# A two-layer decoder trunk: attention pieces counted by matmuls, and stick-breaking sums in fewer, wider matmuls

## The chip, the cores and the metric

The kernel runs on one core of a Trainium2 chip. The metric is the device time of one execution in microseconds (us). The engines that matter are TensorE (PE in the rows; its weight loads are PEld), VectorE (DVE) and ScalarE (ACT). GpSimd (POOL) does very little, and SyncE (SP) only issues the loads of the weights.

## What is computed

`DEPTH` = 2 layers over 256 tokens of width 1024, in float32. A layer has one input projection for three attention branches with 8 heads each, and a squared-ReLU MLP:

```python
proj = hdn @ w_in[l]          # hdn: RMSNorm of x, scaled and shifted by the conditioning
q_lat, c_kv, k_pe, sb_qkv, mb_qkv, gates = split(proj)
q  = rmsnorm(q_lat) @ w_uq[l]      # 768 -> heads of 64 + 32 (rotary)
kv = rmsnorm(c_kv) @ w_ukv[l]      # 256 -> keys (64 a head) and values (64 a head)
o_mla = causal_softmax_attention(q, kv)       # branch A
o_sb  = stick_breaking_attention(sb_qkv)      # branch B
o_mb  = causal_softmax_attention(mb_qkv)      # branch C (at 256 tokens its one block is the own block)
x = x + gate1 * (sum of sigmoid(gates) * (o @ w_o)) @ w_out
x = x + gate2 * squared_relu(hdn2 @ w_ff1) @ w_ff2
```

Stick-breaking attention is `A[t,s] = exp(log_beta[t,s] + sum over s < j < t of log_keep[t,j])`: a sum over the later keys, for each query.

## The kernel before

Activations are held transposed, 128 features on the partitions and 256 tokens along the row. Every product is made of three matmuls on float32 split in a high and a low half (`mm3`, lines 325 to 327: high x high, high x low, low x high). A **job** is one tile of weights of 128 x 2048 at most: SyncE loads it into `ws`, ScalarE rounds it into `wh` (line 168), VectorE subtracts that for `wl` (line 170, 596 of 608 times), in four pieces. Its matmuls are divided into **parts**, most with 24 matmuls of 256 columns. The jobs of a layer, in order: `sb` and `mb` (queries, keys, values of branches B and C), `lat`, `kpe`, the gates of B, **`wukv`**, three jobs **`uq`**, the output projection `osb`, the gates of C, `omb`, the gates of A, `omla`, `wout`, and the MLP. Each third job or so a raw job is put between, in which VectorE makes a conditioning vector of the next section (line 225).

`wukv` has six parts: four make the keys (`ukv`, into the PSUM tile `kn`, copied to `km` by ScalarE at line 700) and two the values (`mla_v`, into `mvps`, copied at line 722). Each of these parts has only 6 matmuls, of 256 columns in `ukv` and of 512 in `mla_v`. A part of a `uq` job has 18, of an output projection 12.

Attention lies between the jobs. Each pair of heads is a Python generator, `sb_attn` or `sm_attn`, that issues a piece of work and then yields how many hand-overs to skip. `run` (line 202) goes through a job's parts; after each it calls `pump`, which lets the two oldest generators make their next piece or count down. For softmax (`sm_attn`) the pieces are: scores `s` with the mask (lines 495 to 501), row maxima and exponentials `e`; two hand-overs later the sums' reciprocals and the scaling of `e` on VectorE (line 518); three later six transposes into `pt` (lines 522 to 524) and the copy `pT`; two later the product with the values into `po` (`av`). For stick-breaking the scores `z` come first, then the log terms `l`, split in `lh` and `ll`; three hand-overs later the sums are added into `z` by matmuls with the triangle `upper` and with `neg_ones` (lines 482 to 486). `drain` in the first `omla` job finishes whatever is left. PSUM tiles of the jobs, `po`, `kn` and `mvps` share three buffers.

The program's order on each engine is made when it is built, and each engine then goes through its instructions in that order.

Of the kernel before, what the change touches and what calls it, by code (L numbers as in the profile page):

```python
# [32 lines left out]
SEAM_N = -3  # L33
WARM = 8, 4, 24
PHASE = 48


@with_exitstack
def trunk(ctx, tc, xT, heads, pos, signs, masks, vecs, gfin, wada, win, wkpe, wuq, wukv, wo, wout, wff1, wff2, out):
# [7 lines left out]
    def mmps(name):  # L47
        return psum.tile([128, 2, 256], F32, name=name, tag="mm", bufs=3)

    def atps(name):  # L50
        return psum.tile([128, 2, 512], F32, name=name, tag="at", bufs=2)
# [4 lines left out]
    def slot(name, dt=F32, shape=(128, 8, 256)):  # L56
        a, b = shape[1:]
        t = big.tile([128, PHASE + 8 * (S + 2)], dt, name=name, tag="slot", bufs=8)
        return t[:, PHASE:PHASE + a * b].rearrange("p (a b) -> p a b", b=b)

# [3 lines left out]
    def t768(name, dt=F32):  # L64
        return work.tile([128, 2, 384], dt, name=name, tag="t768", bufs=4)
# [3 lines left out]

    act = cpool.tile([128, PHASE + 2 * KT * S], F32R, name="act")  # L70
    hh, hl = (act[:, PHASE + i * KT * S:PHASE + (i + 1) * KT * S].rearrange("p (a b) -> p a b", b=S) for i in range(2))
    x = cpool.tile([128, KT, S], F32, name="x")
# [7 lines left out]
    upper, rot_m, rot_b = (csr[:, i, :] for i in range(3))  # L80
    neg_ones = cpool.tile([128, 128], F32R, name="negs")
# [48 lines left out]
    tc.no_sync_barrier()  # L130

    class Job:
        def __init__(self, src, f, parts, raw=False):
            self.src, self.f, self.parts, self.raw = src, f, parts, raw

    jobs = []
    side = []
    state = {"dma": 0, "split": 0, "auto": False}
    PIECES = 4

    def fetch(i):
# [33 lines left out]
    def split_to(i, pc):  # L175
        while state["split"] < min(PIECES * i + pc, PIECES * len(jobs)):
            split_piece()

    def later(i, n):
        while n and i + 1 < len(jobs):  # L180
            i += 1
            n -= not jobs[i].raw
        return i

    def pump():
        for g in list(side[:2]):
            if g[1] > 0:
                g[1] -= 1
                continue
            try:  # L190
                g[1] = next(g[0])
            except StopIteration:
                side.remove(g)
# [8 lines left out]
    def run(i):  # L202
        job = jobs[i]
        if job.raw:
            return
        split_to(i, PIECES)
        n = len(job.parts)
        a = state["split"]
        m = PIECES * (later(i, AHEAD) + 1) - a
        for j, part in enumerate(job.parts):  # L210
            split_to(0, a + m * j // n + (j == 0))
            part(job.wh, job.wl)
            split_to(0, a + m * (j + 1) // n)
            pump()

    def split(dh, dl, src):
        nc.scalar.activation(dh, src, AF.Copy)
        nc.vector.tensor_sub(dl, src, dh.bitcast(F32))  # L218
# [21 lines left out]
    def add_job(job):  # L240
        jobs.append(job)
        every["n"] += 1
        if pending and every["n"] > 0 and every["n"] % every["k"] == 0:
            jobs.append(pending.pop(0)[2])
# [79 lines left out]
    def mm3(o, wh, wl, ah, al, first, last):  # L324
        nc.tensor.matmul(o, wh, ah, start=first, stop=False)  # L325
        nc.tensor.matmul(o, wh, al, start=False, stop=False)  # L326
        nc.tensor.matmul(o, wl, ah, start=False, stop=last)  # L327

    def half(ps, i, wh, wl, kts, ncol, c, ah, al):
        for k in range(kts):  # L330
            c0 = k * ncol + c
            mm3(ps[:, i, :], wh[:, c0:c0 + 128], wl[:, c0:c0 + 128], ah[:, k, :], al[:, k, :],
                k == 0, k == kts - 1)
# [108 lines left out]
    def av(pT, v, p, oh, ol):  # L442
        po = mmps("po")
        for h in range(2):
            d = slice(64 * h, 64 * h + 64)
            vc = slice(p * 128 + 64 * h, p * 128 + 64 * h + 64)
            nc.tensor.matmul(po[d, 0, :], v[:, 0, vc], pT[:, h, 0:256], start=True, stop=False,  # L447
                             tile_position=(0, 64 * h))
        for h in range(2):
            d = slice(64 * h, 64 * h + 64)  # L450
            vc = slice(p * 128 + 64 * h, p * 128 + 64 * h + 64)
            nc.tensor.matmul(po[d, 0, 128:256], v[:, 1, vc], pT[:, h, 256:384], start=False, stop=True,
                             tile_position=(0, 64 * h))
        split(oh[:, p, :], ol[:, p, :], po[:, 0, :])

    def masked(ps, cols, mask, stop):
        nc.tensor.matmul(ps[:, cols], ident_b, mask, start=False, stop=stop, skip_group_check=True)

    def sb_attn(qk, v, p, out):
        z = atps("z")  # L460
        for s in range(2):
            for h in range(2):
                d = slice(64 * h, 64 * h + 64)
                q, k = qk[d, 2 * p, :], qk[d, 2 * p + 1, :]
                if s == 0:
                    nc.tensor.matmul(z[:, h, 0:256], k[:, 0:128], q, start=True, stop=False, skip_group_check=True)
                else:
                    nc.tensor.matmul(z[:, h, 256:384], k[:, 128:256], q[:, 128:256], start=False, stop=False,
                                     skip_group_check=True)
        for h in range(2):  # L470
            for c in (0, 256):
                masked(z[:, h, :], slice(c, c + 128), mask_sb, True)
        l = t768("l")
        zv = z[:, :, 0:384]
        nc.scalar.activation(l, zv, AF.Abs)
        nc.scalar.activation(l, l, AF.Exp, scale=-1.0)
        nc.scalar.activation(l, l, AF.Ln, bias=1.0)
        nc.vector.scalar_tensor_tensor(l, zv, 0.0, l, op0=OP.max, op1=OP.add)
        lh, ll = t768("lh", F32R), t768("ll", F32R)
        split(lh, ll, l)  # L480
        yield 2
        for h in range(2):
            for o, n, w, c in ((0, 256, upper, 0), (128, 128, neg_ones, 256), (256, 128, upper, 256)):
                for t in (lh, ll):
                    nc.tensor.matmul(z[:, h, o:o + n], w, t[:, h, c:c + n], start=False, stop=t is ll,
                                     skip_group_check=True)
        a = t768("a")
        nc.scalar.activation(a, zv, AF.Exp)
        yield 1
        av(a, v, p, *out)  # L490
# [60 lines left out]
    def layer(l):  # L551
# [23 lines left out]
        def start_sb():  # L575
            T["osb"] = otile("osb")
            for p in range(4):
                spawn(sb_attn(T["sbqk"], sbv["v"], p, T["osb"]))
# [125 lines left out]
        def ukv(j, i):  # L704
            def go(wh, wl):
                if i == 0:
                    cell["kn"] = mmps("kn")
                half(cell["kn"], i, wh, wl, 2, 1024, j * 256 + i * 128, T["lh"], T["ll"])
                if i == 1:
                    nope_done("km")(0)(cell["kn"], j)  # L710
            return go

        def mla_v(t):
            def go(wh, wl):
                if t == 0:
                    cell["mv"] = work.tile([128, 2, 512], F32, name="mv", tag="v", bufs=2)
                ps = mmps("mvps")
                for k in range(2):
                    s = slice(k * 1024 + 512, k * 1024 + 1024)
                    mm3(ps, T["lh"][:, k, t * 128:t * 128 + 128], T["ll"][:, k, t * 128:t * 128 + 128],  # L720
                        wh[:, s], wl[:, s], k == 0, k == 1)
                nc.scalar.activation(cell["mv"][:, t, :], ps.rearrange("p a b -> p (a b)"), AF.Copy)
            return go

        add_job(Job(wukv[l], 2048, [ukv(0, 0), ukv(0, 1), ukv(1, 0), ukv(1, 1), mla_v(0), mla_v(1)]))

        def qlat():
            return T["lh"][:, 2:8, :], T["ll"][:, 2:8, :]
# [225 lines left out]
    for l in range(L):  # L954
        layer(l)
# [84 lines left out]
    for i in range(6, len(jobs)):  # L1040
        for f in hooks.get(i, []):
            f()
        if i not in skip:
            run(i)
# [93 lines left out]
```

## Time and profile before

| | us |
|---|---|
| three timed runs | 952.01, 952.58, 953.62 (median 952.58) |
| the profiled execution | 952.03 |
| its span, first to last instruction | 950.2 |
| TensorE matmuls busy | 926.7 (98%), 7839 instructions |
| TensorE weight loads busy | 891.7 (94%) |
| VectorE busy | 742.6 (78%) |
| ScalarE busy | 608.0 (64%) |
| DMA queue q1, share of 16 engines | 60.8% |

The busy time of TensorE is made of matmuls that overlap: the shown duration of one is longer than its distance to the next. So what one costs is read from the starts of neighbours. The mean granted TensorE clock is 0.991 of full speed.

### The profile page before, as it was taken

What the parts mean: (1) busy time and instruction counts of PE and PEld (TensorE: products, weight loads), DVE (VectorE), ACT (ScalarE), POOL (GpSimd) and SP (SyncE); (2) the same over time, 40 slices, a digit from 0 to 9 for tenths busy, and PEclk for the clock granted to TensorE, in tenths of its full rate; (3) what the DMA queues carried; (4) which work ended last, traced back from release to release, by engine and by line L of the source; (5) the groups of instructions that cost most, each with busy time, mean ns of one, the idle gap of its engine ahead of it and who ended that gap; (6) DMA issues with size and microseconds to landing.
All of it is one profiled execution on the core that took longest, in us unless ns stands there. A gap on an engine that the chain in (4) does not pass through costs nothing.

```text
span 950.2 us, 19399 instructions
## 1 busy us (share of the span) xinstructions
PE 926.7 (98%) x7839; PEld 891.7 (94%) x7840; DVE 742.6 (78%) x1438; ACT 608.0 (64%) x1275; POOL 28.3 (3%) x27
## 2 busy tenths in 40 slices
PE   8889999999999999999999999999999999999996
PEld 4889999799999999999999999979999999999995
DVE  7969869797889887667797876979787998555554
ACT  5465678867676775646376657886867678464641
POOL 1510000000000000000000000000000000000002
PEclk9989999999999999999999999999999999999998
DMA  8957556565566488677866565556546647755531
GB/s 328 348 190 260 206 183 216 191 220 195 194 253 238 142 291 308 244 267 264 312 222 245 206 237 178 200 170 227 214 178 223 221 157 266 262 189 197 179 128 44
DMA packets 32920, 208.90 MB, mean 220 GB/s; under 512 B 3776, under 2 KB 4416, under 8 KB 9280
## 3 DMA queue, kind: packets, MB, share of 16 engines
q1 hardware_dynamic: 32688, 207.49, 60.8%
q8 instruction: 61, 1.00, 0.4%
q14 instruction: 27, 0.22, 0.1%
q0 software_dynamic: 144, 0.20, 0.1%
HBM read 206.62 MB, written 1.05 MB: 219 GB/s over the span
## 4 chain that ended last, share of the span: by engine, by line
PE 76%; DVE 15%; DMA 5%; ACT 2%; issue 1%; SPq 0%; DVEq 0%; ACTq 0%
PE ps L325 15%; PE ps L326 15%; PE ps L327 15%; DVE wl L170 5%; PE ff L907 4%; PE ff L910 4%; PE ff L908 4%; PE pre L347 4%; DVE adaw L225 2%; DVE ws L225 2%; DMA ws<-wada 2%; DMA ws<-wff 1%; PE po L447 1%; PE vps L325 1%; PE vps L327 1%
## 5 line engine op out<-in xcount | busy, mean ns | idle before, releaser
L170 DVE TENSOR_TENSOR wl<-ws,wh 128x512 fp32r<-128x512 f32 (+2 forms) x596 | 383.0, 676 | 135.5 <-ACT wh L168 134.8
L168 ACT ACTIVATE wh<-ws 128x512 fp32r<-128x512 f32 (+2 forms) x608 | 344.4, 610 | 194.1 <-PE ps L326 93.5
L325 PE MATMUL ps<-act,wh 128*128 128x256 f32 x1120 | 313.1, 280 | 0.0
L327 PE MATMUL ps<-act,wl 128*128 128x256 f32 x1120 | 310.5, 277 | 0.0
L326 PE MATMUL ps<-act,wh 128*128 128x256 f32 x1120 | 310.5, 277 | 0.0
L325 PEld LDWEIGHTS ps<-act,wh 128*128 128x128 f32 x1120 | 210.4, 188 | 1.3 <-issue 1.0
L326 PEld LDWEIGHTS ps<-act,wh 128*128 128x128 f32 x1120 | 211.2, 189 | 0.2
L327 PEld LDWEIGHTS ps<-act,wl 128*128 128x128 f32 x1120 | 210.2, 188 | 0.0
L907 PE MATMUL ff<-fh,wh 128*128 128x256 f32 x448 | 123.6, 276 | 0.0
L908 PE MATMUL ff<-fl,wh 128*128 128x256 f32 x448 | 123.6, 276 | 0.0
L910 PE MATMUL ff<-fh,wl 128*128 128x256 f32 x448 | 123.6, 276 | 0.0
L225 DVE SCALAR_TENSOR_TENSOR ws<-ws,cb 128x1024 f32<-128x1024 f32 x80 | 95.9, 1220 | 17.0 <-DMA ws<-wada 17.0
L908 PEld LDWEIGHTS ff<-fl,wh 128*128 128x128 f32 x448 | 84.1, 188 | 0.0
L907 PEld LDWEIGHTS ff<-fh,wh 128*128 128x128 f32 x448 | 84.1, 188 | 0.0
L910 PEld LDWEIGHTS ff<-fh,wl 128*128 128x128 f32 x448 | 84.1, 188 | 0.0
L318 ACT ACTIVATE act<-ht,mod 128x256 fp32r<-128x256 f32 x32 | 15.5, 506 | 30.4 <-DVE ht L317 30.4
L421 PE MATMUL first<-act,wh 128*128 128x256 f32 x128 | 27.6, 315 | 7.1 <-ACT act L318 4.6
L774 POOL TENSOR_SCALAR xg<-x,gf 128x256 f32<-128x256 f32 x8 | 8.2, 1033 | 882.4 <-ACT wh L168 873.4
L511 ACT ACTIVATE e<-s,st 128x128 f32<-128x128 f32 (+1 forms) x64 | 26.0, 421 | 11.1 <-DVE st L506 11.0
L421 PEld LDWEIGHTS first<-act,wh 128*128 128x128 f32 x128 | 23.2, 220 | 8.8 <-ACT act L318 5.5
L347 PE MATMUL pre<-xh,wh 128*128 128x258 f32 x96 | 28.3, 294 | 0.0
L326 PE MATMUL ps<-ml,wh 128*128 128x256 f32 x96 | 26.6, 280 | 0.8 <-DVE ml L218 0.8
(261 smaller groups left out, 1862.5 us busy)
## 6 DMA issues: line engine op xcount, KB each, us to landing
ws<-wff SPq DMA_DIRECT2D x64, 1024.0 KB, 4.9
ws<-win SPq DMA_DIRECT2D x50, 1024.0 KB, 4.9
ws<-wada SPq DMA_DIRECT2D x40, 1024.0 KB, 4.9
ws<-wo SPq DMA_DIRECT2D x12, 1024.0 KB, 4.8
adaw<-wada SPq DMA_DIRECT2D x8, 1024.0 KB, 9.1
ws<-wout SPq DMA_DIRECT2D x8, 1024.0 KB, 5.6
ws<-win SPq DMA_DIRECT2D x24, 256.0 KB, 7.9
ws<-wuq SPq DMA_DIRECT2D x6, 768.0 KB, 4.3
```

The source lines that it names most:

```text
L168: nc.scalar.activation(job.wh[:, a], job.ws[:, a], AF.Copy)
L170: eng.tensor_sub(job.wl[:, a], job.ws[:, a], job.wh[:, a].bitcast(F32))
L225: nc.vector.scalar_tensor_tensor(w, w, 1.0, cb, op0=OP.mult, op1=OP.mult, accum_out=mods[l][:, 2 * b + i:2 * b + i + 1])
L325: nc.tensor.matmul(o, wh, ah, start=first, stop=False)
L326: nc.tensor.matmul(o, wh, al, start=False, stop=False)
L327: nc.tensor.matmul(o, wl, ah, start=False, stop=last)
L347: nc.tensor.matmul(ps[:, i, 0:258], w[:, c:c + 128], a[:, k, :], start=k == 0 and n == 0, stop=k == KT - 1 and n == 2, skip_group_check=True)
L421: nc.tensor.matmul(ps[:, i, :], w[:, c:c + 128], a[:, k, :], start=i == 0 and k == 0 and n == 0, stop=k == KT - 1 and n == 2, skip_group_c ...
L511: nc.scalar.activation(e[:, h, a:b], s[:, h, a:b], AF.Exp, scale=scale, bias=st[:, 4 + c:5 + c], accum_out=st[:, 8 + c:9 + c])
L907: nc.tensor.matmul(o, wh[:, c0:c0 + 128], fh[:, k, :], start=st, stop=False, skip_group_check=True)
L908: nc.tensor.matmul(o, wh[:, c0:c0 + 128], fl[:, k, :], start=False, stop=False, skip_group_check=True)
L910: nc.tensor.matmul(o, wl[:, c0:c0 + 128], fh[:, k, :], start=False, stop=en, skip_group_check=True)
```

## The change

There are two edits. A job now knows how many matmuls a part of it has (24, and 6 for `wukv`); `run` adds them up after each part and hands over a piece when 12 have come together, and then starts again from zero. And in the stick-breaking sums the triangle is applied to columns 0 to 383 in one matmul, where it was applied to 0 to 255 and to 256 to 383 in two.

```diff
+PUMP = 12
@@ class Job
-        def __init__(self, src, f, parts, raw=False):
-            self.src, self.f, self.parts, self.raw = src, f, parts, raw
+        def __init__(self, src, f, parts, raw=False, mms=24):
+            self.src, self.f, self.parts, self.raw, self.mms = src, f, parts, raw, mms
@@ run
             part(job.wh, job.wl)
             split_to(0, a + m * (j + 1) // n)
-            pump()
+            state["mms"] += job.mms
+            if state["mms"] >= PUMP:
+                state["mms"] = 0
+                pump()
@@ sb_attn
-            for o, n, w, c in ((0, 256, upper, 0), (128, 128, neg_ones, 256), (256, 128, upper, 256)):
+            for o, n, w, c in ((0, 384, upper, 0), (128, 128, neg_ones, 256)):
                 for t in (lh, ll):
                     nc.tensor.matmul(z[:, h, o:o + n], w, t[:, h, c:c + n], start=False, stop=t is ll,
                                      skip_group_check=True)
@@ layer
-        add_job(Job(wukv[l], 2048, [ukv(0, 0), ukv(0, 1), ukv(1, 0), ukv(1, 1), mla_v(0), mla_v(1)]))
+        add_job(Job(wukv[l], 2048, [ukv(0, 0), ukv(0, 1), ukv(1, 0), ukv(1, 1), mla_v(0), mla_v(1)], mms=6))
```

Lines behind line 212 stand four lower after the change: line 700 of before is 704 of after.

On TensorE, the sums of one head in a stick-breaking pair, with the matmul ahead of them (`csr` holds the triangle, `negs` is `neg_ones`). Before:

```order
L327 MATMUL ps<-act,wl 128x256
L485 MATMUL z<-lh,csr 128x256
L485 MATMUL z<-ll,csr 128x256
L485 MATMUL z<-lh,negs 128x128
L485 MATMUL z<-ll,negs 128x128
L485 MATMUL z<-lh,csr 128x128
L485 MATMUL z<-ll,csr 128x128
```

and after the change:

```order
L331 MATMUL ps<-act,wl 128x256
L489 MATMUL z<-lh,csr 128x384
L489 MATMUL z<-ll,csr 128x384
L489 MATMUL z<-lh,negs 128x128
L489 MATMUL z<-ll,negs 128x128
```

The second head follows with the same rows, so a group of two heads has 12 matmuls before and 8 after; there are four groups in a layer.

On ScalarE, during `wukv` in layer 0 (the numbers tell the tiles of one name apart; `e_1989` and `e_2033` belong to the first and second pair of branch C). Before:

```order
L700 ACTIVATE km_1581<-kn_1998 64x256 x4
L128 ACTIVATE gate_1690<-gate_1690 128x512
L511 ACTIVATE e_1989,st_1985<-s_1976,st_1985 128x128 x2
L511 ACTIVATE e_1989,st_1985<-s_1976,st_1985 128x256 x2
L511 ACTIVATE e_2033,st_2029<-s_2020,st_2029 128x128 x2
L511 ACTIVATE e_2033,st_2029<-s_2020,st_2029 128x256 x2
L700 ACTIVATE km_1581<-kn_2038 64x256 x4
L722 ACTIVATE mv_2062<-mvps_2063 128x512
L526 ACTIVATE pT_2080<-pt_2073 128x768
L722 ACTIVATE mv_2062<-mvps_2082 128x512
L168 ACTIVATE wh_2153<-ws_1966 128x384 x4
```

and after the change, where the pairs are `e_1973` and `e_2036`:

```order
L704 ACTIVATE km_1569<-kn_1982 64x256 x4
L129 ACTIVATE gate_1678<-gate_1678 128x512
L515 ACTIVATE e_1973,st_1969<-s_1960,st_1969 128x128 x2
L515 ACTIVATE e_1973,st_1969<-s_1960,st_1969 128x256 x2
L704 ACTIVATE km_1569<-kn_1999 64x256 x4
L726 ACTIVATE mv_2041<-mvps_2042 128x512
L515 ACTIVATE e_2036,st_2032<-s_2023,st_2032 128x128 x2
L515 ACTIVATE e_2036,st_2032<-s_2023,st_2032 128x256 x2
L726 ACTIVATE mv_2041<-mvps_2052 128x512
L169 ACTIVATE wh_2112<-ws_1950 128x384 x4
```

The second group of `km` copies moved ahead of the second pair's exponentials, and the first pair's `pT` moved out of the stretch; the first `uq` matmul waits for that group of copies in both programs.

On VectorE, in the `uq` and `osb` jobs of layer 0, around the third pair of branch C (`st` its maxima and sums, `qm` the rotary part of the queries). Before:

```order
L170 TENSOR_TENSOR wl<-ws,wh 128x512
L548 TENSOR_TENSOR t_2277<-rp,tab 128x512
L170 TENSOR_TENSOR wl<-ws,wh 128x512
L734 TENSOR_TENSOR t_2169<-t_2169,t_2277 128x512
L514 RECIPROCAL st<-st 128x4
L230 TENSOR_TENSOR mod_89<-mod_89,vec 128x2
L737 COPY qm<-t_2169 32x256 x8
L518 TENSOR_SCALAR e<-e,st 128x128 x2
L518 TENSOR_SCALAR e<-e,st 128x256 x2
```

and after the change:

```order
L741 COPY qm<-t_2128 32x256 x8
L508 TENSOR_REDUCE st<-s 128x2
L509 TENSOR_REDUCE st<-s 128x2
L234 TENSOR_TENSOR mod_89<-mod_89,vec 128x2
L171 TENSOR_TENSOR wl<-ws,wh 128x512
L510 TENSOR_SCALAR st<-st 128x4
L171 TENSOR_TENSOR wl<-ws,wh 128x512 x3
L675 TENSOR_TENSOR merged<-gate,ps 128x512
L518 RECIPROCAL st<-st 128x4
L522 TENSOR_SCALAR e<-e,st 128x128 x2
L522 TENSOR_SCALAR e<-e,st 128x256 x2
```

The third pair's row maxima stood ahead of the `qm` copies and its scaling behind them; now the whole pair stands behind.

## Rows read from the trace of the kernel before

**Rows 1.** The page, first part: busy us (share of the span), instructions.

```profile
PE 926.7 (98%) x7839; PEld 891.7 (94%) x7840; DVE 742.6 (78%) x1438; ACT 608.0 (64%) x1275; POOL 28.3 (3%) x27
```

**Rows 2.** Windows: stretch, its us, busy us of each engine, clock, DMA share, GB/s.

```profile
core 0: us, PE busy (x) PEld busy (x) DVE busy (x) ACT busy (x) POOL busy (x), PEclk, DMA share, GB/s
164.00:175.00 11.00, 9.44 (x69) 7.13 (x68) 9.98 (x29) 10.17 (x34) 0.00 (x0) 1.00 0.78 264
185.00:197.00 12.00, 12.00 (x107) 10.98 (x106) 11.80 (x31) 8.90 (x24) 0.00 (x0) 1.00 0.73 264
```

**Rows 3.** Timeline of PE, layer 0, `wukv` and `uq`: start, us, instruction [idle before].

```profile
169.61 0.47 PE L325 MATMUL mvps<-wh,lath 128*128 128x512 f32 x1
...
170.61 0.39 PE L326 MATMUL mvps<-wl,lath 128*128 128x512 f32 x1
170.84 0.40 PE L327 MATMUL mvps<-wh,latl 128*128 128x512 f32 x1
172.65 0.30 PE L522 MATMUL pt<-head,e 128*128 128x128 f32 x1 [1.41 <-DVE e L518]
...
173.43 0.47 PE L325 MATMUL mvps<-wh,lath 128*128 128x512 f32 x1
...
174.94 0.38 PE L325 MATMUL ps<-lath,wh 128*128 128x256 f32 x1
...
178.00 0.33 PE L522 MATMUL pt<-head,e 128*128 128x128 f32 x1
...
178.63 0.36 PE L325 MATMUL ps<-lath,wh 128*128 128x256 f32 x1
```

**Rows 4.** Timeline of PE, the same place in layer 1.

```profile
625.45 0.40 PE L327 MATMUL mvps<-wh,latl 128*128 128x512 f32 x1
627.15 0.30 PE L522 MATMUL pt<-head,e 128*128 128x128 f32 x1 [1.30 <-DVE e L518]
...
628.04 0.48 PE L325 MATMUL mvps<-wh,lath 128*128 128x512 f32 x1
```

**Rows 5.** Timeline of ACT, layer 0: the second group of `km` copies.

```profile
173.33 1.57 ACT L700 ACTIVATE km<-kn 64x256 f32<-64x256 f32 x4
```

**Rows 6.** The chain that ended last, in order of time: start, us, what.

```profile
144.55 0.64 ACT wh L168
...
168.40 0.46 DVE wl L170
168.86 0.61 DVE gate L127
...
169.50 0.63 ACT gate L128
...
170.14 1.73 ACT e L511 x8
```

**Rows 7.** Timeline of PE: one group of stick-breaking sums, and the matmul behind it.

```profile
110.46 0.28 PE L485 MATMUL z<-lh,csr 128*128 128x256 f32 x1
110.58 0.28 PE L485 MATMUL z<-ll,csr 128*128 128x256 f32 x1
110.70 0.22 PE L485 MATMUL z<-lh,negs 128*128 128x128 f32 x1
110.75 0.28 PE L485 MATMUL z<-ll,negs 128*128 128x128 f32 x1
...
111.09 0.33 PE L485 MATMUL z<-lh,csr 128*128 128x256 f32 x1
...
111.78 0.33 PE L325 MATMUL ps<-act,wh 128*128 128x256 f32 x1
```

**Rows 8.** Timeline of PE: the third pair's scores and its transposes.

```profile
186.10 0.49 PE L495 MATMUL s<-mbqk 64*128 64x128 f32 x4
...
187.16 0.36 PE L325 MATMUL ps<-lath,wh 128*128 128x256 f32 x1
...
197.26 0.27 PE L522 MATMUL pt<-head,e 128*128 128x128 f32 x1
```

**Rows 9.** Timeline of DVE: the scaling of the third pair.

```profile
195.21 1.01 DVE L518 TENSOR_SCALAR e<-e,st 128x128 f32<-128x128 f32 x4
```

More of the change, by code (lines that the diff above doesn't have):

```diff
@@ L132, in trunk @@
     class Job:
-        def __init__(self, src, f, parts, raw=False):
-            self.src, self.f, self.parts, self.raw = src, f, parts, raw
+        def __init__(self, src, f, parts, raw=False, mms=24):
+            self.src, self.f, self.parts, self.raw, self.mms = src, f, parts, raw, mms
     jobs = []
     side = []
-    state = {"dma": 0, "split": 0, "auto": False}
+    state = {"dma": 0, "split": 0, "auto": False, "mms": 0}
     PIECES = 4
```

## The prediction

> **What bounds the kernel now.** I read the busy shares first. TensorE's matmul row is busy for 98% of the span and its weight loads for 94%, VectorE for 78% [rows 1]. So the time is TensorE's instruction stream plus the holes in it, and a change is worth the stream time it removes and the holes it closes, as long as nothing else is late instead. The granted clock is 1.00 in the stretches looked at [rows 2], the one with the hole included, so nothing is to be had or lost there.
>
> Then I read the holes. In the steady part there are two alike, one a layer. In layer 0 the sixth `mvps` matmul starts at 170.84 and the first transpose `pt` at 172.65, after 1.41 us of idle time that ended with a VectorE scaling of `e` [rows 3]; the next `mvps` matmul starts 2.59 us after the sixth. Undisturbed, a 512-column matmul takes 0.23 (170.61 to 170.84) and six transposes take 0.63 (178.00 to 178.63) [rows 3], together 0.86, so the hole costs 1.7 us. In layer 1 the same two matmuls stand 2.59 us apart again (625.45 and 628.04), with 1.30 us of idle time shown [rows 4]. The hole sits in the job `wukv`, whose six parts have 6 matmuls each: a piece of attention was handed over after every part, so softmax and transpose of one head pair came only a few microseconds after its scores.
>
> Behind it stands VectorE: 9.98 of 11.00 us busy in that stretch [rows 2]. The chain of waits leaves TensorE at 144.55, runs through VectorE to the gate operation at 168.86, and from there over ScalarE's exponentials to the transposes [rows 6].
>
> **Part 1: pieces by matmul count.** Only `wukv` changes its rate: every other job keeps the default 24, over the limit of 12, so it hands over a piece per part as before. In `wukv` three hand-overs of six go, in each layer. No instruction is removed; what comes later is moved past.
>
> The hole at `pt` closes: the 36 matmuls of the first `uq` job now stand ahead of the transposes, which puts them some 4 us behind the end of `wukv`, while the scaling that they waited for was done by 172.65 [rows 3]. But a new wait takes part of its place, and it can be read from the order. The first matmul of `uq`, the job behind `wukv`, writes a PSUM buffer that the second group of `km` copies must have emptied. TensorE reaches `mvps` as before (the same matmuls and two score blocks stand ahead), at 169.61 or up to 0.3 earlier; twelve at 0.23 take 2.8 us, so it wants `uq` at 172.1 to 172.4. ScalarE does in order: gate from 169.50 for 0.63, four exponentials 1.73 [rows 6], then the four copies 1.57 [rows 5]. That ends at 173.4, or at 173.0 if the gate operation on VectorE comes earlier, since one weight split of 0.46 [rows 6] now stands behind it and not ahead. I take 173.2. Before, `uq` started at 174.94 [rows 3] with the six transposes done; they still have to be done later, at 0.63. Gain in a layer: 174.94 - 173.2 - 0.63 = 1.1 us, of which the new wait has eaten about 1. If ScalarE did not bind, 172.2 gives 2.1; if VectorE's part is half a microsecond late, 0.6. For two layers: **2.2 us, between 1.2 and 4.2**. I take the middle one because the copies stand behind the exponentials in the order as built.
>
> What else moves: in each layer all later attention pieces of both softmax branches come three hand-overs later, their ScalarE and VectorE work with them. They then run into the second of the gate jobs behind `omb`, and five parts stay free ahead of the drain at `omla`, so no piece is left to be done in a row with nothing beside it. No DMA is issued in a piece, and SyncE and GpSimd keep their order.
>
> **Part 2: one matmul of 384 columns.** A group (one of 8, four a layer) has 12 matmuls before and 8 after, over the same 2048 columns. Rows: 110.46 to 111.78, so 1.32 us for 12, 0.63 for the first head and 0.69 for the second [rows 7]. A 256-column matmul takes 0.12; the first of 128 takes 0.05, but from the second to the next head 0.34 pass for three, 0.11 each [rows 7]: a matmul as narrow as that does not get below what its weight load needs. The four that go are of this kind, and the four widened ones grow. A 384-column matmul is not in the trace; between 0.12 for 256 and 0.23 for 512 I take 0.175. Head after: 2 x 0.175 + 0.05 + 0.11 = 0.51, or 0.57 with the 0.06 that the second head has more. A group costs 1.02 to 1.14 and saves 0.18 to 0.30; I take 0.25. Of the four groups in a layer, one stands in the stretch in which VectorE sets the pace (144.55 to 168.86), where a TensorE that is early only waits longer. Six count: **1.5 us, between 1.1 and 2.4** (all eight at 0.30).
>
> One rule speaks against this part. Rows 7 show 1.32 us for 2048 columns, more than the 0.96 that eight times 0.12 would give. The Trainium skill, TensorE: Matmul & The Clock Gate, section Step-by-step: what each phase is for, says of the streaming phase "This is why throughput is purely `N cycles`", so 2048 columns would cost the same in 12 matmuls as in 8 and part 2 would bring nothing. The trace does not agree where the matmuls have 128 columns; by the rule the sum would be 2.2 and not 3.7.
>
> **Sum.** 2.2 + 1.5 = 3.7 us less. The profiled run took 952.03, its span 950.2 and 1.8 around it, and would become 948.3. The four runs known are 952.01, 952.03, 952.58 and 953.62, their middle 952.3; for the median I predict 952.3 - 3.7 = **948.6**.
>
> **Rivals.**
> (a) ScalarE does not bind and the whole hole closes: 4.2 + 2.0 = 6.2 less, 946.1. For it: ScalarE is off the path elsewhere. Against: the order puts the copies behind the exponentials.
> (b) The columns alone count and part 2 brings nothing: 952.3 - 2.2 = 950.1.
> (c) Given back: VectorE is full again right behind, 11.80 of 12.00 us [rows 2]. If the moved pieces only make TensorE wait there for what it gained, or the new wait is as long as the old, the time stays at 951 to 953. Against: in that stretch TensorE is busy all 12 us, so its work is ready ahead of it.
> (d) Slower, by one mechanism: transposes that wait in the jobs `osb`. The third pair's scores started at 186.10, and the first scaling was through a quarter of its 1.01 us from 195.21, 9.4 us later; its transposes came at 197.26 [rows 8, 9]. After the change the same distance, counted in the order, is 60 matmuls at 0.115 to 0.12, the score block itself and another (1.06 each, 186.10 to 187.16), six transposes and an `av` block: at least 10 us. So there is about 1 us of room. It decides if scores to scaled `e` takes over 13 us: then 3 us are lost in a layer, 6 in all, and the time is 952.3 - 3.7 + 6 = 954.6. For it: full VectorE. Against: in the new order this pair's reductions stand behind the eight `qm` copies (2.4 us of the 9.4 before) and its scaling is no longer queued behind them.
> (e) That the change doesn't do what it says: the order shows that it does.
>
> **How the numbers follow.** Forecast 0.61; (a) 0.12; (b) 0.05; (c) 0.14; (d) 0.08. The measurement tells about 0.2%, 1.9 us, from no change, so (b), 2.2 less, is split between faster (0.03) and same (0.02), and 0.02 of the forecast falls to same with the low ends of both parts. Faster 0.61 - 0.02 + 0.12 + 0.03 = 0.74; same 0.14 + 0.02 + 0.02 = 0.18; slower 0.08. The range takes in the forecast with its own ends (952.3 less 2.3 to 6.6 at the most, 945.7 to 950.0), (a), (b) and the near end of (c), and cuts the far tail below 946: 946.0 to 951.2.
>
> **What would show it.** Right: no idle time ahead of any `pt`; about 1 us of idle ahead of the first `uq` matmul (`ps<-lath`) in each layer, ended by ScalarE's `km`; the first `uq` matmul some 3.8 us after the first `mvps` matmul, not 5.3 (169.61 to 174.94 [rows 3]); a z group of 1.02 to 1.14 us. Wrong: idle time ahead of `pt` in the `osb` jobs (d), z groups still at 1.3 (b), or TensorE's idle time after layer 0's `wukv` grown by what was won (c). The forecast falls if `km` takes TensorE past 174, or if a PSUM buffer that I did not follow is late.

## The result, and the profile after

The changed kernel takes 959.26 us (median of 7 runs, 956.56 to 960.98) against 952.58 for the kernel before (7 runs beside them): ratio 1.0061, 95% interval 1.0041 to 1.0082. (The ratio compares means, 958.86 and 953.03, and not medians.) That is 6.7 us slower in the medians and 5.8 in the means where 3.7 us faster was forecast, and outside the range. The profiled execution took 957.26 against 952.03, so 5.2 us have to be found between the two traces. Lines of code from the attention functions on stand four numbers later than before (L447 is now L451).

Two views of before, asked again. TensorE's busy row, from the page's first part, which answers [rows 1]: the same number of busy microseconds in a longer span.

```profile
span 955.5 us, 19334 instructions
PE 926.6 (97%) x7808; PEld 891.7 (93%) x7808; DVE 741.7 (78%) x1438; ACT 608.2 (64%) x1275; POOL 28.4 (3%) x27
```

So the loss is idle time. The two windows of [rows 2] show where (stretch, its us, busy us of PE, PEld, DVE, ACT, POOL, granted clock, DMA share, GB/s):

```profile
164.00:175.00 11.00, 9.74 (x74) 7.82 (x73) 9.41 (x26) 10.43 (x33) 0.00 (x0) 1.00 0.70 249
185.00:197.00 12.00, 9.51 (x82) 8.76 (x80) 11.83 (x29) 7.74 (x21) 0.00 (x0) 1.00 0.61 234
```

The first window, with `wukv` in it, has gained 0.3 us of work. The second, in which TensorE had been busy all 12 us, now has 2.5 us of idle time.

**What came as forecast.** At the end of `wukv` in layer 0 (timeline of PE: start, us, instruction, idle time ahead and who ended it; answers [rows 3]) no transpose `pt` interrupts the `mvps` matmuls any more, and the first `uq` matmul waits for ScalarE's `km` copies, at 173.66 where 173.2 was forecast:

```profile
172.31 0.39 PE L330 MATMUL mvps<-wl,lath 128*128 128x512 f32 x1
172.53 0.40 PE L331 MATMUL mvps<-wh,latl 128*128 128x512 f32 x1
173.66 0.38 PE L329 MATMUL ps<-lath,wh 128*128 128x256 f32 x1 [0.74 <-ACT km L704]
```

The wait costs 1.13 - 0.23 = 0.90 us, and in layer 1 as much. A group of stick-breaking sums (answers [rows 7]) takes 111.57 - 110.48 = 1.09 us and not 1.32; a 384-column matmul takes 0.17:

```profile
110.48 0.34 PE L489 MATMUL z<-lh,csr 128*128 128x384 f32 x1
110.65 0.34 PE L489 MATMUL z<-ll,csr 128*128 128x384 f32 x1
110.82 0.22 PE L489 MATMUL z<-lh,negs 128*128 128x128 f32 x1
...
111.57 0.33 PE L329 MATMUL ps<-act,wh 128*128 128x256 f32 x1
```

**What no row of before had shown.** In the `osb` jobs of both layers TensorE stops ahead of a `po` block, the product of the transposed weights `pT` with `v`. Timeline of PE, layer 0, then layer 1:

```profile
191.50 0.27 PE L528 MATMUL pt<-head,e 128*128 128x128 f32 x1
...
194.23 0.28 PE L331 MATMUL ps<-osb,wl 128*128 128x256 f32 x1
197.13 0.65 PE L451 MATMUL po<-pT,v 128*64 128x256 f32 x4 [2.62 <-ACT pT L530]
...
649.74 0.28 PE L331 MATMUL ps<-osb,wl 128*128 128x256 f32 x1
652.81 1.12 PE L451 MATMUL po<-pT,v 128*64 128x256 f32 x4 [2.80 <-ACT pT L530]
```

From one matmul to the next 2.90 and 3.07 us pass where 0.21 would do, as in the kernel before (182.84 to 183.05 in the rows below): 2.69 + 2.86 = 5.55 us, more than the whole difference by itself. The `pT` that is waited for is the second pair's. Its six transposes started at 190.95 to 191.50; ScalarE copied them at 196.26. Here is what ScalarE did in between, and behind it VectorE (timelines of ACT and DVE; the rows of the accumulator reads on ACT are left out):

```profile
190.38 1.66 ACT L169 ACTIVATE wh<-ws 128x512 fp32r<-128x512 f32 x3
194.66 0.37 ACT L515 ACTIVATE e<-s,st 128x128 f32<-128x128 f32 x1 [2.62 <-DVE st L510]
...
195.81 0.48 ACT L515 ACTIVATE e<-s,st 128x256 f32<-128x256 f32 x1
...
196.26 0.82 ACT L530 ACTIVATE pT<-pt 128x768 f32<-128x768 f32 x1
```

```profile
190.27 2.38 DVE L741 COPY qm<-t 32x256 f32<-32x256 f32 x8
192.67 0.42 DVE L508 TENSOR_REDUCE st<-s 128x2 f32<-128x256 f32 x1
193.01 0.68 DVE L509 TENSOR_REDUCE st<-s 128x2 f32<-128x512 f32 x1
193.72 0.16 DVE L234 TENSOR_TENSOR mod<-mod,vec 128x2 f32<-128x2 f32 x1
193.80 0.68 DVE L171 TENSOR_TENSOR wl<-ws,wh 128x512 fp32r<-128x512 f32 x1
194.40 0.16 DVE L510 TENSOR_SCALAR st<-st 128x4 f32<-128x4 f32 x1
```

ScalarE went through its instructions in the order of the program, and in that order the four exponentials `e` of the third pair stand ahead of the copy. They need the third pair's row maxima, which VectorE reaches only behind eight `qm` copies. So ScalarE stands idle for 2.62 us with a copy in its queue that could have run soon after 191.5. In the kernel before, the second pair was three hand-overs further on: its `pT` copy ran at 178.91, its `po` at 183.05, long before the third pair's exponentials at 190.35. Timelines of before, ACT and then PE:

```profile
178.91 0.81 ACT L526 ACTIVATE pT<-pt 128x768 f32<-128x768 f32 x1 [0.29 <-PE pt L524]
...
190.35 0.37 ACT L511 ACTIVATE e<-s,st 128x128 f32<-128x128 f32 x1 [0.56 <-DVE st L506]
```

```profile
182.84 0.28 PE L327 MATMUL ps<-lath,wl 128*128 128x256 f32 x1
183.05 0.65 PE L447 MATMUL po<-pT,v 128*64 128x256 f32 x4
```

**The clock.** Behind the hole in layer 1 the granted clock fell from 1.00 to 0.50 (2.4 to 1.2 GHz); behind the one in layer 0 it did not. Windows of PE alone, in layer 1: stretch, us, PE busy and number of instructions, clock, DMA share, GB/s.

```profile
652.81:656.00 3.19, 3.19 (x16) 0.50 0.88 303
657.00:660.00 3.00, 3.00 (x31) 1.00 0.00 0
```

From the start of `po` to the start of the 40th matmul from there 4.45 us pass in layer 0 and 6.03 in layer 1: 1.58 us lost to the clock.

**The sum.** Closing the `pt` holes gives 1.7 (below); the columns 1.2 (first experiment); the two `po` holes cost 5.55, three smaller waits for `pT` (0.21, 0.20 and 0.15 us, at 205, 243 and 663) 0.56, the clock 1.58. Together 4.8 slower, against 5.2 between the two profiled runs. That they come so close is partly luck, since small terms of both signs are left out. Where the loss lies can be seen without the sum: set beside each other matmul by matmul, the changed kernel stands 0.0 us behind at 153, 2.8 behind at 288, 0.4 at 622 and 5.1 at 717 (times of before). So it loses in the attention pieces of both layers and wins 2.4 back in between (the columns of layer 1 among it, an estimated 0.9: four groups at 1.32 - 1.09).

The runs lie at 956.6 to 957.3 with a mean clock of 0.990 to 0.992, and at 959.3 to 961.0 with 0.987 to 0.989. A fall of the clock in both layers would fit the later ones, but no trace of one was taken, and there is a rival. Near 78 us, long before the change acts on `wukv`, the clock fell in six of the fourteen traces of this text (the runs e1, e3, v4, v6, p1 and t1 below), though not in the three of the kernel before and the changed kernel. Windows of PE, first the kernel with the columns alone (e1), then before:

```profile
78.72:82.13 3.41, 3.41 (x18) 0.50 0.65 250
```

```profile
78.70:82.00 3.30, 3.30 (x31) 1.00 0.51 206
```

Between 78.5 and 80.3 us the first of these fell 1.5 us behind. So single executions can differ by that much for a reason that has nothing to do with the holes at `po`.

### The profile page after: what moved, and what is told of

Same layout as the page of the kernel before. It is cut to its first block, busy times and chain, and to the rows that moved or that the text cites. A ratio compares the mean times of both kernels' runs of the same rounds, so it can differ in the third digit from the quotient of the medians.

```text
span 955.5 us, 19334 instructions
## 1 busy us (share of the span) xinstructions
PE 926.6 (97%) x7808; PEld 891.7 (93%) x7808; DVE 741.7 (78%) x1438; ACT 608.2 (64%) x1275; POOL 28.4 (3%) x27
## 3 DMA queue, kind: packets, MB, share of 16 engines
HBM read 206.62 MB, written 1.05 MB: 217 GB/s over the span
## 4 chain that ended last, share of the span: by engine, by line
PE 73%; DVE 13%; DMA 6%; ACT 4%; issue 2%; POOL 1%; SPq 0%; DVEq 0%; ACTq 0%; POOLq 0%
PE ps L329 14%; PE ps L330 13%; PE ps L331 13%; PE ff L914 5%; PE ff L911 5%; PE ff L912 5%; DVE wl L171 5%; PE pre L351 4%; DMA ws<-wada 2%; DVE ws L229 2%; ACT e L515 2%; DMA ws<-win 2%; PE po L451 1%; PE vps L329 1%; PE vps L331 1%
```

## The experiments

Theory A: the loss is part 1's alone; it is the place of the second pair's `pT` copy in ScalarE's queue, behind exponentials that wait for VectorE, and the clock behind the hole. Theory B: part 2 is at fault. Rival C: the copy is late for a reason of its own. Every ratio below is to the kernel before, timed beside the kernel in question.

**Each part alone.** The kernel before with the wide matmul:

```
-for o, n, w, c in ((0, 256, upper, 0), (128, 128, neg_ones, 256), (256, 128, upper, 256)):
+for o, n, w, c in ((0, 384, upper, 0), (128, 128, neg_ones, 256)):
```

> The kernel before with the 384-column matmul alone; pieces are still handed over per part. Theory A (the loss comes from the pacing: the pT copy of the second pair stands on ScalarE behind the third pair's exponentials, which wait for VectorE): no po hole over 0.5 us in the osb jobs, the pt holes of 1.3 to 1.4 us ahead of the transposes are still there, a z group 1.09 instead of 1.32, of which part is absorbed: 0.4 to 1.5 us less than before, 951 to 952. Theory B (the wide matmul brings work forward that is then missed, or is slow in itself): 3 us or more over before, 956 and up, with the po holes there.

952.31 us (12 runs) against 953.37: ratio 0.9987, interval 0.9975 to 1.0000. No `po` hole; the `pt` holes are there. So part 2 gave 1.2 us (0 to 2.4, hardly clear of noise), as theory A has it.

The changed kernel with the three narrow matmuls:

> The pacing by matmul count alone, with the three old matmuls in the stick-breaking sums. Theory A: the po holes of 2.8 and 2.96 us stand again in the osb jobs of both layers, the time is that of the changed kernel plus the 0.4 to 1.5 us that the columns had saved, 958 to 962. Theory B: no po hole, 950 to 951 as the prediction had it for part 1. On the clock: if a hole of this size makes it fall, the granted clock shows 0.5 for some 3 us behind the hole in one layer or in both; if what was seen in one execution was chance, it stays at 1.00.

960.05 us (6 runs), ratio 1.0071, interval 1.0053 to 1.0088. The matmuls ahead of `po` and `po` itself stand 2.72 and 2.77 us apart, and the clock fell behind the second, not the first. Timeline of PE in layer 0:

```profile
194.74 0.28 PE L331 MATMUL ps<-osb,wl 128*128 128x256 f32 x1
197.46 0.65 PE L451 MATMUL po<-pT,v 128*64 128x256 f32 x4 [2.44 <-ACT pT L530]
```

Theory B is out: the pacing alone costs 6.7 us.

**VectorE's queue.** The changed kernel with the `qm` copies on another engine:

```
-nc.vector.tensor_copy(T["qm"][64:96, 4 * i + h, :], raw[32 * h:32 * h + 32, i, :])
+nc.gpsimd.tensor_copy(T["qm"][64:96, 4 * i + h, :], raw[32 * h:32 * h + 32, i, :])
```

> The changed kernel with the eight qm copies moved from VectorE to GpSimd, which takes 2.4 us of queue from ahead of the third pair's row maxima. Theory A: the maxima come some 2 us earlier, the po hole shrinks from 2.8 to under 1 us, the clock stays at 1.00 behind it, and the time is 3 to 6 us under the changed kernel, 951 to 955. Rival C (the pT copy is late for a reason of its own on ScalarE, not through VectorE): the hole stays over 2.3 us and the time within 1 us of the changed kernel. If the copies are slow on GpSimd, the scores that read qm show it as a new wait of their own.

954.64 us (10 runs), ratio 1.0010, interval 0.9996 to 1.0024. Timeline of PE at the hole in layer 0:

```profile
195.47 0.28 PE L331 MATMUL ps<-osb,wl 128*128 128x256 f32 x1
196.94 0.65 PE L451 MATMUL po<-pT,v 128*64 128x256 f32 x4 [1.20 <-ACT pT L530]
```

The hole went from 2.90 to 1.47 us (layer 1: 3.07 to 1.60), and behind it the clock stayed at 1.00 in both layers. (This execution stood 1.24 us later already at the first `uq` matmul, 174.90 against 173.66, so distances are compared and not the times themselves.) "Under 1 us" was too much to ask: the maxima stood 1.56 us ahead of the last matmul before the hole (192.67 to 194.23) and now stand 3.18 ahead (192.29 to 195.47), 1.6 us earlier and not 2.4, because a `mod` operation and a weight split now come before them on VectorE. GpSimd needs 5.42 us for the eight copies and nobody waits for them. The control, the same move in the kernel before:

> The kernel before with the qm copies on GpSimd and nothing else: a control for the run that moved them in the changed kernel. If that run gained because its hole hung on VectorE's queue (theory A), there is no hole of this kind here and the time is that of before within 1 us, 952.5 to 953.5. If VectorE's 2.4 us are worth something anywhere, as the same gain of some 4.6 us would show, it is 949 or less.

954.30 us against 953.31 (12 and 23 runs), ratio 1.0008, interval 0.9995 to 1.0020. Where no hole hangs on VectorE's queue, taking 2.4 us from it gains nothing.

**ScalarE's queue.** The changed kernel with the copy of that one pair on VectorE:

```
+if p == 1 and scale == 0.125:
+    nc.vector.tensor_copy(pT, pt[:, :, 0:384])
+else:
     nc.scalar.activation(pT, pt[:, :, 0:384], AF.Copy)
```

> The changed kernel with one copy moved: the pT copy of the second pair of the omb branch on VectorE, where it stands behind the third pair's maxima and one weight split, and no longer on ScalarE behind the third pair's exponentials. Theory A (the copy waits for its place in a queue, the transposes having ended long before, at 191.7): it starts at about 195.2 and not at 196.3, the po hole becomes 1.7 to 2.1 us, the clock stays at 1.00 behind it, and the time is 2 to 4 us under the changed kernel, 955 to 957.5. If the copy waited for the transposes or for its buffer, the hole stays at 2.8 or more.

954.99 us (12 runs), ratio 1.0019, interval 1.0005 to 1.0033. Timeline of DVE in layer 0, then of PE in layer 0 and in layer 1:

```profile
195.85 0.95 DVE L531 COPY pT<-pt 128x768 f32<-128x768 f32 x1
```

```profile
195.25 0.28 PE L331 MATMUL ps<-osb,wl 128*128 128x256 f32 x1
196.94 0.44 PE L451 MATMUL po<-pT,v 128*64 128x256 f32 x2 [1.42 <-DVE pT L531]
...
649.95 0.28 PE L331 MATMUL ps<-osb,wl 128*128 128x256 f32 x1
652.40 0.70 PE L451 MATMUL po<-pT,v 128*64 128x256 f32 x2 [2.17 <-DVE pT L531]
```

Only the engine and with it the queue of this copy was changed (VectorE takes 0.95 us for it, ScalarE 0.82), and the hole shrank to 1.69 and 2.45 us. Rival C, a copy late for a reason of its own, is out. Layer 1 kept more of its hole than expected, and the clock fell there behind 2.45 us (window 653 to 654):

```profile
653.00:654.00 1.00, 1.00 (x9) 0.50 0.00 0
```

The traced execution took 957.59, one of the slowest of the twelve; the clock fell in it near 78 us too. By the medians the kernel is 4.1 us under the changed kernel timed in the same group (959.14, below), more than the 1.83 us that the two holes gave back. That the clock held in most executions would fit, but no trace of one was taken.

**The order.** The changed kernel with the two `mvps` parts counted at 12 matmuls each (`run` then takes the count of the part), so four hand-overs in `wukv` and not three:

```
-add_job(Job(wukv[l], 2048, [...], mms=6))
+add_job(Job(wukv[l], 2048, [...], mms=[6, 6, 6, 6, 12, 12]))
```

> The changed kernel with the two mvps parts counted at their 12 matmuls each: four hand-overs in wukv and not three, which in ScalarE's order puts the pT copy of the second pair ahead of the third pair's exponentials. Theory A: no po hole over 0.5 us in the osb jobs, no clock drop, the pt hole in wukv stays closed, and the time is 4 to 8 us under the changed kernel: 949 to 952.5. Rival C: the po hole is still there whatever the order, 956 or more. Rival D (the four hand-overs bring the pt hole of before back, since the transposes come earlier again): 1.3 us of idle ahead of pt in each layer and 951 to 953.

952.63 us (12 runs), ratio 0.9986, interval 0.9975 to 0.9997. One hand-over turns the order round. Timeline of ACT, layer 0, without the accumulator reads:

```profile
189.06 0.82 ACT L530 ACTIVATE pT<-pt 128x768 f32<-128x768 f32 x1
...
195.70 0.37 ACT L515 ACTIVATE e<-s,st 128x128 f32<-128x128 f32 x1 [1.42 <-DVE st L510]
```

ScalarE still waits for VectorE, but the second pair's copy is through by 189.88 and its `po` runs without a wait at 193.27. The `pt` hole stayed closed (rival D out). What was missed: the next pair has the same trouble in small, a `po` hole of 1.05 us at 204 and one of 1.44 in layer 1:

```profile
657.31 0.28 PE L331 MATMUL ps<-osb,wl 128*128 128x256 f32 x1
658.75 0.44 PE L451 MATMUL po<-pT,v 128*64 128x256 f32 x2 [1.16 <-ACT pT L530]
```

With the `qm` copies on GpSimd as well:

> Four hand-overs in wukv and the qm copies on GpSimd, with the 384-column matmul. By theory A the rest of the loss of the four hand-overs, po holes of 0.93 us at 204 and 1.33 at 657, is VectorE's backlog too and goes to under 0.4 each; the km wait of 0.91 in each layer stays. Then 1 to 2 us under the kernel with four hand-overs alone, 950.5 to 952. If those holes have another cause they stay, and the time is the same within 0.5 us.

951.17 us (12 runs), ratio 0.9983, interval 0.9970 to 0.9996; no `po` block waits for `pT` any more. The copies were worth nothing in the kernel before and are worth these holes here.

**The clock.** The changed kernel with matmuls that fill the hole:

```
 po = mmps("po")
+for _ in range(fill):        # 22 for the second pair of omb, else 0
+    nc.tensor.matmul(po[:, 1, 0:128], ident_b, mask_sm, start=True, stop=True, ...)
```

> The changed kernel with 22 extra 128-column matmuls, whose output nobody reads, ahead of the second pair's po block in the osb jobs of both layers, so that TensorE works through most of the hole. If the drop of the clock behind the hole is a cost of its own (theory A, second part): po starts no earlier than in the changed kernel (some 2.9 to 3.1 us behind the matmul before the hole, or up to 0.3 more), the granted clock stays at 1.00 behind it in both layers, and the time is 1.5 to 3.5 us under the changed kernel, 955.5 to 957.5, in one bunch and not two. If the clock costs nothing that is felt at the end: the time of the changed kernel, 957 to 961.

958.07 us (6 runs), ratio 1.0052, interval 1.0035 to 1.0069. The 22 matmuls took only 1.2 us (0.055 each), so 1.6 us of hole are left:

```profile
649.83 0.33 PE L449 MATMUL po<-msk 128*128 128x128 bf16 x3
651.54 0.65 PE L453 MATMUL po<-pT,v 128*64 128x256 f32 x4 [1.38 <-ACT pT L532]
```

```profile
653.00:654.00 1.00, 1.00 (x11) 1.00 0.98 418
```

The clock did not fall, and from the start of `po` to the 40th matmul from there 4.46 us pass in both layers. The profiled run took 955.38, 1.9 less than that of the changed kernel. But the median lies above the 955.5 to 957.5 that were expected, and can't be told from the changed kernel's (959.26, and 959.14 below). So the cost of the clock is shown in the traces and not in the times.

**The changed kernel again.**

> The changed kernel once more, unaltered, beside the other two of this group. If its loss is what the first trace shows (po holes of 2.8 to 3.0 us in both layers, km waits of 0.9, and a clock that falls behind the hole in one layer or both), the holes are there again within 0.3 us and the time is 957 to 961, 5 to 7 us over before. If the first trace was an accident of one execution, the holes differ by more.

959.14 us (6 runs), ratio 1.0058, interval 1.0038 to 1.0079; the distances at `po` are 2.85 and 2.98 us, the clock fell in layer 1 and not in layer 0. Windows of PE, layer 0 and layer 1:

```profile
198.00:199.00 1.00, 1.00 (x9) 1.00 0.78 295
654.00:655.00 1.00, 1.00 (x7) 0.50 0.95 401
```

**The `km` wait.** The kernel with four hand-overs and `qm` on GpSimd still pays 0.90 us in each layer for the wait that the prediction had seen. ScalarE's four copies of a group as two:

```
-nc.scalar.activation(T[key][0:64, 4 * (u + j) + 2 * i + h, :], ps[64 * h:64 * h + 64, i, :], AF.Copy)
-for i in range(2) for h in range(2)]
+nc.scalar.activation(T[key][0:64, 4 * (u + j) + h:4 * (u + j) + h + 3:2, :], ps[64 * h:64 * h + 64, :, :], AF.Copy)
+for h in range(2)]
```

> Four hand-overs, the qm copies on GpSimd, and the four km copies of a group (and the four of qm that ScalarE makes) as two of 64x512 in place of four of 64x256, at an estimated 0.57 each by a weight copy of 128x512 in the trace, so 1.1 and not 1.5 us. If the first uq matmul waits for the km copies and nothing else, its wait shrinks from 0.90 to about 0.5 us in each layer, and the time is 0.5 to 1 us under the kernel without this, 950 to 951. If something else is ready no earlier, the wait stays at 0.9.

950.27 us (12 runs) against 953.90, ratio 0.9964, interval 0.9952 to 0.9977: the fastest of all, 3.4 us under the kernel before. The new copies, from the rows of their line (nanoseconds: minimum, median, maximum):

```profile
L704 ACT ACTIVATE km<-kn x8: 582/593/595, 167.4 to 623.9; 64x512 f32<-64x512 f32 x8
```

A group takes 1.2 us. The wait fell to 0.60 in layer 1 but only to 0.86 in layer 0, where the gate operation, the exponentials and the copies started later against TensorE. So the wait explains 0.3 us of the gain over the kernel without this (0.9 in the medians); the rest stays open. Last, the same kernel with a hand-over per part, as before the change:

> The last kernel (384 columns, qm copies on GpSimd, km copies as two of 64x512) with the pieces handed over per part again, six hand-overs in wukv. If four hand-overs are worth what the traces show (the pt holes of 1.47 to 1.57 us in each layer closed, a km wait of 0.6 to 0.9 in their place), it is 1 to 2.5 us over the last kernel, 951 to 953, with pt holes of 1.2 us or more. If the pacing is worth nothing in any form and the gain came from the shorter copies, it is within 0.5 us of it, 950 to 951.

951.48 us (12 runs), ratio 0.9989, interval 0.9971 to 1.0006, with `pt` holes of 1.46 and 1.51 us. Four hand-overs are 1.2 us better in the medians, 2.4 by the two ratios and 0.8 in the profiled runs. The two intervals overlap by a little, so this gain is likely but not certain.

**A miss.** The kernel with four hand-overs and the last `po` block of each layer done twice:

```
+po = mmps("again")      # behind the last pair: the four matmuls of av once more, unread
```

> The kernel with four hand-overs and, behind the last po block of each layer, the same four matmuls once more into a buffer that nobody reads. The traces show two rates of the steady 256-column stream, 113.3 and 117.8 ns a matmul, and most po blocks end in the other rate than they began in; with four hand-overs the stretches 258 to 294 and 712 to 748 run at 117.8. If a po block flips the rate, these stretches run at 113.3, which gives 1.35 us back in each layer for 0.8 us of work: 0.5 to 1.5 us under the kernel with four hand-overs. If the rate hangs on something else there (the weights' place, the PSUM buffers), it stays at 117.8 and the time is 1.6 us over it.

957.74 us (5 runs), ratio 1.0047, interval 1.0035 to 1.0059, beyond the dearer of the two expectations. Behind the doubled block the stream ran at 117.8 ns a matmul in layer 0 and at 113.3 in layer 1. The third pair's `po` hole in layer 1 was 2.23 us and not 1.44; why is open (the extra block also takes a turn of the three `mm` buffers). Of the 4.2 us between the traced executions of the two kernels, 1.1 stood ahead of the first doubled block already (first `mvps` matmul of layer 0 at 172.62 and not 171.48); the loss as a whole is not explained. What it says of the two rates stands at the end.

## Why the prediction was wrong

**The reading of before was right.** The holes at `pt` were where it put them, they closed, and the `km` wait took their place at about its forecast price (0.90 against 1.0). The gain in a layer: 2.59 - 0.23 = 2.36 us were lost ahead of the seventh `mvps` matmul [rows 3, 4]; of these 0.63 are the transposes, done later, and 0.90 the new wait. That leaves 0.83, so 1.7 in both layers where the sum had 2.2. One reading was a little off: TensorE did not reach `mvps` in layer 0 at 169.61 or earlier but at 169.93, after a wait of 0.52 us for VectorE; from there to `uq` it took 3.73 us where about 3.8 was forecast.

**Part 2 came out near its forecast**: 1.2 us measured (0 to 2.4), 1.5 forecast, and in the trace a group at 1.09, inside the forecast 1.02 to 1.14. By the trace rival (b) falls with it; the time alone would not rule it out. That six of eight groups count was not borne out in layer 0 of these two traces: the changed kernel was 0.43 us ahead at 125.6 and level again at 153. The rule of the Trainium skill that was weighed there (TensorE: Matmul & The Clock Gate, Step-by-step: what each phase is for) does not hold for matmuls as narrow as 128 columns: the same 2048 columns take 1.32 us in 12 matmuls and 1.09 in 8.

**The step that failed is "What else moves".** It said that the attention pieces come three hand-overs later and asked only whether any would be left over at the drain; in rival (d), whether the third pair's transposes would find their scaled `e` ready. They did: scores at 188.41, scaling from 197.08, transposes without a wait at 202.04. But the delay is not the same for all pairs. The second pair came three hand-overs later and met the third, and two pairs that had run on either side of the weight work now shared ScalarE's queue in the wrong order. For each moved instruction the question had to be what stands ahead of it on its own engine, and what that waits for. The prediction asked this of `km` and of `pt`, not of `pT`. It was `pT` that came late: for it TensorE stood idle 2.62 and 2.80 us ahead of the second pair's `po`, a wait to which the sum gave nothing. Rival (d) had the right place, engine and size (3 us in a layer) and the wrong instruction (so that its size came out was luck); its 954.6 left out the clock. At 0.08 its chance was too small: against it the prediction had put that the third pair's reductions stand behind the `qm` copies, counting only what this does to the third pair's own transposes, and that place was the cause.

**The clock** was set aside because it was 1.00 in the stretches of before, the hole included. That held for holes of 1.8 and 1.7 us from matmul to matmul (170.84 to 172.65 [rows 3], 625.45 to 627.15 [rows 4]), 1.3 to 1.4 of it idle. A change that can open a longer hole can also lose the clock, here 1.58 us.

**What it took for granted** and what held: no idle time ahead of `pt` in `wukv`, no DMA touched, VectorE's full stretch behind. The last was read as harmless, since TensorE was busy all 12 us [rows 2]. It was so only while nothing that TensorE needed soon stood behind it.

## What to carry to other kernels

When a change delays a chain by some hand-overs, write down for each engine the new order of all the steps of the neighbouring chains. Ask of every step that stands behind another chain's step what that one waits for: a short copy that was free can inherit the wait of a whole queue. An engine that is full but waited for by nobody is a hole that has not opened yet.

## What the runs showed of the hardware

**A hole and the clock.** The length of the hole alone does not decide whether the clock falls. Ahead of `po` it stayed at 1.00 behind 2.72, 2.85 and 2.90 us in layer 0, and fell to 0.50 behind 2.45, 2.77, 2.98 and 3.07 us in layer 1 (distances from matmul to matmul, four traces). In layer 1 it did not fall behind 2.23 us (the doubled block's run), and behind 1.05 to 1.69 us it fell in neither layer. What else differs between the cases stays open.

**Two rates of the same stream.** The long runs of 256-column matmuls go at 113.3 or at 117.8 ns each, at a granted clock of 1.00 either way, and mostly stay at one rate until another kind of block or a short wait comes between. The two executions of the changed kernel have the same order of instructions on TensorE and differ in this. Timeline of PE in the same jobs, first execution and second:

```profile
274.75 0.28 PE L330 MATMUL ps<-act,wh 128*128 128x256 f32 x1
...
275.43 0.28 PE L330 MATMUL ps<-act,wh 128*128 128x256 f32 x1
```

```profile
274.73 0.28 PE L329 MATMUL ps<-act,wh 128*128 128x256 f32 x1
...
275.43 0.28 PE L329 MATMUL ps<-act,wh 128*128 128x256 f32 x1
```

The two rows are six matmuls apart, 0.68 us (113 ns each) in the first and 0.70 (117) in the second. Counted over all fourteen traces (nine matmuls on either side, and nothing but such matmuls for 13 on either side), a `po` block leaves at the other rate than it found in 194 of 202 cases. The doubled block flipped the rate once and not twice (from 113.3 to 117.8 in layer 0, from 117.8 to 113.3 in layer 1), so it is the passage through such a block and not the number of its matmuls. A stretch of 36 us at the slower rate costs 1.4 us by these two figures, so the rate is one reason why executions of one kernel differ by some microseconds. What sets it is open.
